# Softmax of differential attention over whole rows of scores, with the recurrent heads on one bank of PSUM

## The chip, the cores and the metric

The kernel runs on one core of a Trainium2 chip. The metric is the time of one execution on the device, in microseconds; a kernel's time is the median of its runs. Its engines are named as in the profile: PE (TensorE, matmuls; PEld is its weight load), DVE (VectorE), ACT (ScalarE), POOL (GpSimd) and SP (SyncE, which issues the DMAs). PSUM has eight banks; one bank holds 512 float32 columns of 128 rows.

## The reference

One encoder layer over two groups of rows, 2048 (prompt) and 256 (sample), width 1024. A projection feeds two mixers: differential attention with 4 heads, and a bidirectional recurrence (RWKV7) with 8 heads of 64. Their outputs are joined, projected (`w_out`), added to the input and passed through an MLP of width 4096. The part that the change touches:

```python
def one_block(q_blk):                                  # 128 queries, all keys of the sequence
    s = jnp.einsum("bqhcd,bkhcd->bhcqk", q_blk, k) * scale
    p = jax.nn.softmax(s, axis=-1)                     # c: the two maps of a head
    attn = p[:, :, 0] - lam * p[:, :, 1]
    return jnp.einsum("bhqk,bkhe->bqhe", attn, v)
o = rms_norm(o, subln_g) * (1.0 - lambda_init)
```

## The kernel before

`build` runs three stages: the projections with the recurrence's preparation, then attention and the recurrent units together, then `wout` and `mlp`. In the second stage `merge` pulls from two generators: one step of `attn_stream` (277 in all), then as many of `rw_units` (126) as keep pace. That gives the order of the program's text; a scheduling pass of the framework reorders instructions by its own timing of them and their priority, and then each engine executes its queue strictly in order. A tile from a pool with `bufs=n` has n slots; whoever needs a slot waits until its last reader is done.

`attn_stream` goes over 72 items: 4 heads, and in each 16 query tiles of the long sequence and 2 of the short one. A long item has 16 key tiles, in `nh` = 4 groups of `HB` = 4 tiles (512 columns). For each group and each of the two maps `attn_scores` (L581) does two matmuls into one bank `sc` (pool `asp`, `SC` = 3 slots of one bank), the negated maximum on DVE (L591) and the exponential on ACT with that group's own maximum as bias and the row sum as accumulator output (L595). Behind each group of scores stands `attn_pv` (L628) for the item before: four transposes into the one bank `atp` (L632), a copy on ACT (L634), and products with `vv` into `oo` (L637), whose one bank holds two items' outputs side by side.

Since each group has its own maximum, `attn_combine` (L598) makes up for it: the maximum over the groups (L604), the correction `cf` (L605, L606), corrected sums (L607, L608), the factor `g` of the second map for each group (L610 to L613). Then, for each group, it scales the first map's `P` by `cf` (L618 on ACT for the groups in `SCA`, L620 on POOL for the others) and adds the second map times `g` (L626 on DVE, or L623 and L624 on POOL for the groups in `STP`). `attn_out` (L639) norms the output: sum of squares on ACT (L643), two operations of one column on DVE (L645, L646), a power on POOL (L647), the scaling on DVE (L649), and the store.

The recurrent units: `rw_inter` (L875, once per unit and direction, 36 calls) makes from the prepared tensors the decays, the operands `ar` and `bk`, the scores `sc` (L935, evicted and masked by DVE at L938) and the transposed `bkt` (L941, evicted by ACT at L942); `rw_leaf` (L948) inverts small triangular blocks by 31 dependent steps (L962, L964) on DVE and POOL, between two transfers through DRAM (MD, XD); `rw_merge` (L968) puts the inverses together; `rw_chain` (L1025) runs the recurrence itself, whose output `yp` (L1016) is gathered over the whole of a step and copied by ACT (L1082). Its PSUM: the tag `w` with `WB` = 2 banks serves `lp` (L894), `scp`, `bp` and `yp`; the tag `ch` has one bank. So the eight banks are 3 for `sc`, one each for `atp` and `oo`, 2 for `w`, one for `ch`.

In `rw_inter` the scores take both banks at once:

```python
pss = [pp.tile([128, 4, 128], F32, name="scp", tag=SCPT, bufs=WB) for h in range(2)]
for c in range(4):
    for h in range(2):
        ...
        nc.tensor.matmul(pss[h][:, c], ...)
for h in range(2):
    nc.vector.tensor_tensor(out=sc[:, h, 4 * x:4 * x + 4], in0=pss[h], ...)
```

## Time and profile before

| | us |
|---|---|
| median of 3 runs (lowest, highest) | 4062.52 (4062.09, 4064.07) |
| the profiled execution | 4069.43 |
| its span, first to last instruction | 4067.6 |
| first and last score matmul (L588) begin at | 828.3 and 2170.1 |
| last product of attention (L637) begins at | 2193.7 |

| busy over the whole span | PE | PEld | DVE | ACT | POOL |
|---|---|---|---|---|---|
| us | 3841.0 | 3428.7 | 2535.4 | 1904.9 | 1249.5 |
| share | 94% | 84% | 62% | 47% | 31% |

The profile is of one execution. A share over the whole span mixes three stages; what concerns the change is read from the stretch between about 830 and 2195 us. PE's busy time is modelled from pipelined matmuls and contains some waiting; PEld beside it helps to judge it. A group's row gives busy time, the mean of one instruction, and the engine's idle time just before it with what ended that. The chain of waits is followed back from the last instruction, at each step to what released it or to the instruction before it on its engine.

### The profile page before, as it was taken

Reading aid. Unit: us, or ns where it says so; the run is one execution under the profiler, and the core shown is the slowest. Engines: PE = TensorE matmul, PEld = TensorE weight load, DVE = VectorE, ACT = ScalarE, POOL = GpSimd, SP = SyncE. Lnnn points to the kernel's source line nnn. Section 1 sums busy time; section 2 is a strip of 40 time slices with the busy share of each in tenths; the row PEclk is TensorE's granted clock in tenths of the full one; section 3 lists DMA queues with packets and bytes.
Section 4 is the critical chain, followed back from the end, with each engine's and each line's share of the span. In section 5 each row is a group of like instructions: output and inputs, shape, how many; then the busy total and the mean of one; then the engine's idle time right before and its main releaser. Section 6 shows DMA issues by size and latency. Waiting matters only on the chain.

```text
span 4067.6 us, 75970 instructions
## 1 busy us (share of the span) xinstructions
PE 3841.0 (94%) x28790; PEld 3428.7 (84%) x28790; DVE 2535.4 (62%) x5080; ACT 1904.9 (47%) x4312; POOL 1249.5 (31%) x1632
## 2 busy tenths in 40 slices
PE   8999998988889888889897999999999999999999
PEld 8999998976777677777776778999999999999998
DVE  4254767679878878788885775444444444444443
ACT  4354555467666656566665224333333333333332
POOL 0023666556656556556554440000000000000000
PEclk9999998999989989889998999999999999999999
DMA  6366666643443343334324376222252222521221
GB/s 188 121 198 194 199 178 195 181 108 73 111 95 83 94 119 90 85 85 112 89 62 151 105 234 200 63 68 67 63 186 63 64 66 65 158 63 63 63 63 39
DMA packets 617558, 458.05 MB, mean 113 GB/s; under 512 B 232498, under 2 KB 569191, under 8 KB 617192
## 3 DMA queue, kind: packets, MB, share of 16 engines
q1 hardware_dynamic: 617192, 453.20, 38.9%
q8 instruction: 227, 3.72, 0.4%
q14 instruction: 139, 1.14, 0.1%
HBM read 323.98 MB, written 129.07 MB: 111 GB/s over the span
## 4 chain that ended last, share of the span: by engine, by line
PE 54%; DVE 11%; POOL 6%; DMA 4%; issue 3%; ACT 2%; SPq 1%; POOLq 0%; DVEq 0%; ACTq 0%
PE ups L102 7%; PE ups L100 7%; PE ups L101 7%; PE yps L102 6%; PE yps L101 6%; PE yps L100 6%; DVE nb L591 2%; PE oo L637 2%; PE wops L101 2%; PE wops L100 2%; PE wops L102 2%; POOL lx L964 1%; DMA XD<-lx 1%; POOL ltmp L962 1%; DVE lx L964 1%
## 5 line engine op out<-in xcount | busy, mean ns | idle before, releaser
L504 DVE TENSOR_TENSOR acc<-yps,acc 128x512 f32<-128x512 f32 x576 | 392.0, 688 | 374.8 <-PE yps L102 374.8
L100 PE MATMUL ups<-h2hi,f_hi 128*128 128x384 f32 x1536 | 515.6, 336 | 0.0
L102 PE MATMUL ups<-h2hi,f_lo 128*128 128x384 f32 x1536 | 515.6, 336 | 0.0
L101 PE MATMUL ups<-h2lo,f_hi 128*128 128x384 f32 x1536 | 515.3, 335 | 0.0
L595 ACT ACTIVATE P<-sc,nb 128x512 f32<-128x512 f32 (+1 forms) x528 | 360.2, 685 | 218.4 <-DVE nb L591 203.2
L101 PE MATMUL yps<-f_lo,uh 128*128 128x512 f32 x1152 | 449.8, 391 | 0.0
L100 PE MATMUL yps<-f_hi,uh 128*128 128x512 f32 x1152 | 449.6, 391 | 0.0
L102 PE MATMUL yps<-f_hi,ul 128*128 128x512 f32 x1152 | 442.8, 391 | 0.0
L137 ACT CAST f_hi<-f_raw 128x1024 fp32r<-128x1024 f32 x96 | 96.2, 1048 | 646.7 <-PE yps L102 645.3
L591 DVE TENSOR_REDUCE nb<-sc 128x1 f32<-128x512 f32 (+1 forms) x528 | 345.2, 671 | 56.7 <-PE sc L589 55.6
L637 PE MATMUL oo<-vv,at 128*128 128x128 f32 x2080 | 307.0, 294 | 31.5 <-ACT at L634 20.6
L637 PEld LDWEIGHTS oo<-vv,at 128*128 128x128 f32 x2080 | 272.1, 202 | 60.9 <-ACT at L634 31.6
L588 PE MATMUL sc<-kt,qq 128*128 128x512 f32 (+1 forms) x528 | 253.3, 480 | 49.0 <-ACT P L595 42.1
L492 DVE TENSOR_TENSOR ul<-u,uh 128x384 fp32r<-128x384 f32 x192 | 106.8, 556 | 299.8 <-ACT uh L491 296.3
L101 PEld LDWEIGHTS ups<-h2lo,f_hi 128*128 128x128 f32 x1536 | 288.2, 188 | 5.7
L102 PEld LDWEIGHTS ups<-h2hi,f_lo 128*128 128x128 f32 x1536 | 288.2, 188 | 5.5
L100 PEld LDWEIGHTS ups<-h2hi,f_hi 128*128 128x128 f32 x1536 | 288.3, 188 | 5.5
L102 PEld LDWEIGHTS yps<-f_hi,ul 128*128 128x128 f32 x1152 | 216.1, 188 | 47.4
L143 DVE SCALAR_TENSOR_TENSOR f_lo<-f_raw,g,f_hi 128x256 fp32r<-128x256 f32 x384 | 168.7, 481 | 138.6 <-ACT f_hi L142 138.5
L100 PE MATMUL mm<-w_hi,hT_hi 128*128 128x256 f32 x864 | 250.2, 290 | 4.9 <-DVE qn L330 4.2
L100 PEld LDWEIGHTS yps<-f_hi,uh 128*128 128x128 f32 x1152 | 216.3, 188 | 39.3
L101 PE MATMUL mm<-w_lo,hT_hi 128*128 128x256 f32 x864 | 249.0, 289 | 0.0
(236 smaller groups left out, 9313.0 us busy)
## 6 DMA issues: line engine op xcount, KB each, us to landing
f_raw<-w_ff SPq DMA_DIRECT2D x192, 256.0 KB
f_raw<-w_ff SPq DMA_DIRECT2D x96, 512.0 KB
w_raw<-w_in SPq DMA_DIRECT2D x104, 256.0 KB
qq<-QT SPq DMA_DIRECT2D x288, 64.0 KB
kb<-KB SPq DMA_DIRECT2D x36, 512.0 KB
ZT<-zs SPq DMA_DIRECT2D x84, 192.0 KB
xt<-x SPq DMA_DIRECT2D x27, 512.0 KB
zr<-ZT SPq DMA_DIRECT2D x18, 516.0 KB
```

The source lines that it names most:

```text
L100: mm(ps, lh, rh, start=start, stop=False)
L101: mm(ps, lh, rl, start=False, stop=False)
L102: mm(ps, ll, rh, start=False, stop=stop)
L137: nc.scalar.copy(hi[:, ks], raw)
L143: nc.vector.scalar_tensor_tensor(out=lo[:, k], in0=raw[:, k - k0], scalar=gk, in1=hi[:, k].bitcast(F32), op0=ALU.mult, op1=ALU.subtract)
L492: nc.vector.tensor_tensor(out=ul[:, ns], in0=u2, in1=uh[:, ns].bitcast(F32), op=ALU.subtract)
L504: nc.vector.tensor_tensor(out=acc[j][:, cs], in0=ps, in1=acc[j][:, cs], op=ALU.add)
L588: nc.tensor.matmul(sc, qq[:, c, 0], kt, start=True, stop=False)
L591: nc.vector.tensor_reduce(out=m, in_=sc, axis=AX.X, op=ALU.max, negate=True)
L595: nc.scalar.activation(out=P, in_=sc, func=AF.Exp, bias=m, accum_out=(a["ls"][:, hf] if a["nh"] > 1 else a["l"])[:, c:c + 1])
L637: nc.tensor.matmul(a["op"], at[:, b], a["kv"][1][hf][:, b], start=k == 0, stop=k == a["n"] - 1)
L964: e.tensor_tensor(out=X[:, 0:i, k0:16], in0=X[:, 0:i, k0:16], in1=tmp[:, 0:i, 0:n], op=ALU.add)
```

## The change

Attention works on one map at a time over all its columns. `asp` gets two slots of two banks; `attn_scores(a, c)` fills both for map `c` (8 matmuls, 2048 columns), takes two maxima over 1024 columns and the minimum of the two negated values, and only then two exponentials of 1024 columns with the row's own bias. So nothing is rescaled: `cf` and all that makes and applies it is gone. `attn_combine` makes one factor `g` for the row; the first 512 columns are combined by DVE, the others of the second map are scaled by ACT in place and added by POOL, 512 columns at a time. In `attn_out` the two small operations go to POOL and the last scaling to ACT. `attn_pv` works as before on pieces of the wider tiles, and `attn_stream` puts two groups of products behind each map's scores. The probabilities are held in 4 and 2 tiles of 1024 columns (`PA`, `PB`) in place of 6 and 6 of 512.

Four banks for scores, with `atp`, `oo` and `ch`, leave one: `WB` becomes 1, and `rw_inter` does the scores of one half, evicts them, then the other half.

```diff
@@ attn_pools
-        self.asp = ctx.enter_context(tc.tile_pool(name="asp", bufs=SC, space=PSUM, side="right"))
+        self.asp = ctx.enter_context(tc.tile_pool(name="asp", bufs=2, space=PSUM, side="right"))
@@ attn_scores
-    def attn_scores(self, a, hf):
+    def attn_scores(self, a, c):
...
+        m = a["mx"] if nj > 1 else nb[:, :, 0]
+        scs = []
+        for j in range(nj):
+            sc = self.asp.tile([128, NB2, HW], F32, name="sc", tag="sc")
+            for b in range(NB2):
+                kt = a["kv"][0][c][j * NB2 + b]
+                nc.tensor.matmul(sc[:, b], qq[:, c, 0], kt, start=True, stop=False)
+                nc.tensor.matmul(sc[:, b], qq[:, c, 1], kt, start=False, stop=True)
+            sc = sc.rearrange("p b k -> p (b k)")
+            nc.vector.tensor_reduce(out=nb[:, c, j:j + 1], in_=sc, axis=AX.X, op=ALU.max, negate=True)
+            scs.append(sc)
+        if nj > 1:
+            nc.vector.tensor_reduce(out=m[:, c:c + 1], in_=nb[:, c], axis=AX.X, op=ALU.min)
+        for j in range(nj):
+            P = a["P"][c][j] = sp.tile([128, NB2 * HW], F32, name=f"P{c}", tag=f"P{c}", bufs=(PA, PB)[c])
+            nc.scalar.activation(out=P, in_=scs[j], func=AF.Exp, bias=m[:, c:c + 1],
+                                 accum_out=a["ls"][:, c, j:j + 1] if nj > 1 else a["l"][:, c:c + 1])
@@ attn_combine
...
+        if nj > 1:
+            nc.vector.tensor_reduce(out=l, in_=a["ls"], axis=AX.X, op=ALU.add)
+        nc.vector.reciprocal(g, l[:, 1:2])
+        nc.vector.scalar_tensor_tensor(out=g, in0=g, scalar=l[:, 0:1], in1=self.neglam, op0=ALU.mult, op1=ALU.mult)
+        for j in range(nj):
+            A, B = a["P"][0][j], a["P"][1][j]
+            k0 = 0
+            if j == 0:
+                nc.vector.scalar_tensor_tensor(out=A[:, 0:HW], in0=B[:, 0:HW], scalar=g, in1=A[:, 0:HW], op0=ALU.mult, op1=ALU.add)
+                k0 = HW
+            if k0 < NB2 * HW:
+                nc.scalar.activation(out=B[:, k0:], in_=B[:, k0:], func=AF.Copy, scale=g)
+            for k in range(k0, NB2 * HW, HW):
+                nc.gpsimd.tensor_tensor(out=A[:, k:k + HW], in0=A[:, k:k + HW], in1=B[:, k:k + HW], op=ALU.add)
@@ attn_out
-        nc.vector.scalar_tensor_tensor(out=rs, in0=l0, scalar=1e-6, in1=l0, op0=ALU.mult, op1=ALU.mult)
-        nc.vector.scalar_tensor_tensor(out=rs, in0=ss, scalar=1.0 / 128, in1=rs, op0=ALU.mult, op1=ALU.add)
+        nc.gpsimd.tensor_scalar(out=rs, in0=l0, scalar1=l0, scalar2=1e-6, op0=ALU.mult, op1=ALU.mult)
+        nc.gpsimd.tensor_scalar(out=rs, in0=ss, scalar1=1.0 / 128, scalar2=rs, op0=ALU.mult, op1=ALU.add)
...
-        nc.vector.tensor_scalar(out=o, in0=op, scalar1=rs, scalar2=None, op0=ALU.mult)
+        nc.scalar.activation(out=o, in_=op, func=AF.Copy, scale=rs)
@@ attn_stream
-            for hf in range(max(x["nh"] for x in (prev, cur) if x)):
-                if cur and hf < cur["nh"]:
-                    self.attn_scores(cur, hf)
-                if prev and hf < prev["nh"]:
-                    self.attn_pv(prev, hf)
-                yield
+            nh = max(x["nh"] for x in (prev, cur) if x)
+            for c in range(2):
+                if cur:
+                    self.attn_scores(cur, c)
+                for hf in range(c * nh // 2, (c + 1) * nh // 2) if nh > 1 else range(c):
+                    if prev and hf < prev["nh"]:
+                        self.attn_pv(prev, hf)
...
+                    yield
@@ rw_inter
-            pss = [pp.tile([128, 4, 128], F32, name="scp", tag=SCPT, bufs=WB) for h in range(2)]
-            for c in range(4):
-                for h in range(2):
-                    hs = slice(h * 64, h * 64 + 64)
...
+            for h in range(2):
+                hs = slice(h * 64, h * 64 + 64)
+                ps = pp.tile([128, 4, 128], F32, name="scp", tag=SCPT, bufs=WB)
+                for c in range(4):
+                    nc.tensor.matmul(ps[:, c], bk[hs, c, x].rearrange("p s t -> p (s t)"),
...
+                nc.vector.tensor_tensor(out=sc[:, h, 4 * x:4 * x + 4], in0=ps, in1=self.mask[:, d * (1 + h):d * (1 + h) + 1].to_broadcast([128, 4, 128]), op=ALU.mult)
@@ constants
-WB = 2
+WB = 1
-PA = 6
-PB = 6
+PA = 4
+PB = 2
```

## Rows read from the trace of the kernel before

**Rows 1.** windows, 900 to 2190 us: busy time of each engine (instructions), granted clock, DMA share, GB/s
```profile
900.00:2190.00 1290.00, 1136.99 (x13383) 944.54 (x13382) 1056.51 (x2398) 840.19 (x2098) 759.90 (x1125) 0.93 0.37 90
```

**Rows 2.** chain of waits, 900 to 2190 us, share by line, cut by the view
```profile
by line: issue 8.6%; DVE nb L591 6.9%; PE oo L637 5.0%; POOL lx L964 4.2%; DMA XD<-lx 4.1%; POOL ltmp L962 3.9%; DVE lx L964 3.7%; DVE ltmp L962 3.6%; DVE P L626 3.5%; POOL P L624 3.0%; PE scp L935 2.9%; PE sc L588 2.7%; PE atp L632 2.3%; A
```

**Rows 3.** groups by line, DVE, attention: busy us, mean ns | idle before, releasers
```profile
L591 DVE TENSOR_REDUCE nb<-sc 128x1 f32<-128x512 f32 x512 | 339.2, 679 | 52.4 <-PE sc L589 51.5
...
L591 DVE TENSOR_REDUCE nb<-sc 128x1 f32<-128x256 f32 x16 | 6.1, 411 | 4.3 <-PE sc L589 4.2
...
L626 DVE SCALAR_TENSOR_TENSOR P<-P,g,P 128x512 f32<-128x512 f32 (+1 forms) x136 | 135.3, 1029 | 2.9
...
L604 DVE TENSOR_REDUCE mx<-nb 128x2 f32<-128x8 f32 x64 | 9.5, 148 | 0.4
...
L605 DVE TENSOR_TENSOR cf<-mx,nb 128x8 f32<-128x8 f32 x64 | 13.4, 210 | 0.6
...
L607 DVE TENSOR_TENSOR ls<-ls,cf 128x8 f32<-128x8 f32 x64 | 17.6, 275 | 12.9 <-ACT cf L606 10.1 <-ACT P L595 2.2
...
L613 DVE TENSOR_SCALAR g<-cf,g 128x4 f32<-128x4 f32 x64 | 19.5, 304 | 1.0
...
L645 DVE SCALAR_TENSOR_TENSOR ors<-l 128x1 f32<-128x1 f32 x72 | 17.5, 244 | 0.1
...
L646 DVE SCALAR_TENSOR_TENSOR ors<-oss,ors 128x1 f32<-128x1 f32 x72 | 19.2, 267 | 18.5 <-ACT osq L643 18.1
...
L649 DVE TENSOR_SCALAR o<-oo,ors 128x128 f32<-128x128 f32 x72 | 24.6, 342 | 13.5 <-POOL ors L647 11.3 <-DMA MIX<-o 1.9
```

**Rows 4.** the same view, ACT
```profile
L595 ACT ACTIVATE P<-sc,nb 128x512 f32<-128x512 f32 (+1 forms) x528 | 360.2, 685 | 218.4 <-DVE nb L591 203.2 <-DVE P L626 4.6 <-POOL ors L647 3.6
...
L595 ACT ACTIVATION_READ_ACCUMULATOR P<-sc,nb 128x1 f32 x528 | 106.2, 201 | 0.0
...
L618 ACT ACTIVATE P<-P,cf 128x512 f32<-128x512 f32 x128 | 85.6, 717 | 1.4
...
L375 ACT ACTIVATE wo_hi<-acc,subg 128x1024 fp32r<-128x1024 f32 x4 | 4.6, 1149 | 4.0 <-DMA acc<-w_out 3.8
```

**Rows 5.** the same view, POOL
```profile
L624 POOL TENSOR_TENSOR P<-P,P 128x512 f32<-128x512 f32 x128 | 182.0, 1440 | 0.1
...
L623 POOL TENSOR_SCALAR P<-P,g 128x512 f32<-128x512 f32 x128 | 126.7, 1001 | 54.4 <-DVE g L613 35.8 <-DVE ors L646 9.3 <-ACT bkt L942 3.1
...
L620 POOL TENSOR_SCALAR P<-P,cf 128x512 f32<-128x512 f32 x128 | 98.3, 777 | 163.4 <-ACT cf L606 148.7 <-issue 9.9 <-ACT P L595 1.9
...
L647 POOL TENSOR_TENSOR ors<-ors,halfneg 128x1 f32<-128x1 f32 x72 | 42.6, 592 | 119.3 <-DVE ors L646 116.3 <-DVE lx L964 1.7 <-DVE g L610 0.8
```

**Rows 6.** waits, 828 to 2195 us: total us, times, longest us
```profile
PE sc L588 <- ACT P L595: 42.1, 35, 3.6
...
PE bp L941 <- DVE sc L938: 14.4, 13, 2.5
```

**Rows 7.** timeline, 1500 to 1545 us, rw_inter and one yp: start us, us, instruction
```profile
1511.25 0.91 PE L1016 MATMUL yp<-S,ar 64*64 64x64 f32 x22
...
1513.87 1.16 PE L894 MATMUL lp<-tw,wup 65*128 65x128 f32 x8
...
1525.22 0.56 ACT L1082 COPY ys<-yp 128x512 f32<-128x512 f32 x1
...
1530.74 1.16 PE L935 MATMUL scp<-ar,bk 64*128 64x128 f32 x16
...
1536.11 0.96 PEld L935 LDWEIGHTS scp<-ar,bk 64*128 64x128 f32 x8 [0.37 <-DVE zt L984]
...
1537.60 0.67 DVE L938 TENSOR_TENSOR sc<-scp,mask 128x512 f32<-128x512 f32 x1
...
1540.10 0.66 PE L941 MATMUL bp<-ident,bk 128*128 128x128 f32 x4
...
1541.15 0.59 ACT L942 COPY bkt<-bp 128x512 f32<-128x512 f32 x1
```

More of the change, by code (lines that the diff above doesn't have):

```diff
@@ L573, in attn_begin @@
                 nc.sync.dma_start(out=qq[64 * r:64 * r + 64, c].bitcast(F32), in_=self.QT[2 * h + c, :, :, t0:t0 + 128])
-        a = dict(h=h, t0=t0, HB=HB, nh=nh, n=n, kv=kv, qq=qq, P=[[None] * nh for _ in range(2)], op=self.oo[:, par])
-        for nm, shape in (("nb", [128, nh, 2]), ("ls", [128, nh, 2]), ("l", [128, 2]), ("g", [128, nh]), ("mx", [128, 2])):
+        a = dict(h=h, t0=t0, HB=HB, nh=nh, NB2=NB2, nj=nj, n=n, kv=kv, qq=qq, P=[[None] * nj for _ in range(2)], op=self.oo[:, par])
+        for nm, shape in (("nb", [128, 2, nj]), ("mx", [128, 2]), ("ls", [128, 2, nj]), ("l", [128, 2]), ("g", [128, 1])):
@@ L576, in attn_begin @@
             a[nm] = sp.tile(shape, F32, name=nm, tag="a" + nm)
[L577 to L578 removed]
         return a
[L581 removed]
+    def attn_scores(self, a, c):
         nc, sp = self.nc, self.aw
[L584 to L596 removed]
+        HW, nb, qq, nj, NB2 = a["HB"] * 128, a["nb"], a["qq"], a["nj"], a["NB2"]
+        m = a["mx"] if nj > 1 else nb[:, :, 0]
[15 more added lines that the diff above has]
+                                 accum_out=a["ls"][:, c, j:j + 1] if nj > 1 else a["l"][:, c:c + 1])
@@ L609, in attn_combine @@
-        gl = g[:, nh - 1:nh]
-        nc.vector.reciprocal(gl, l[:, 1:2])
-        nc.vector.scalar_tensor_tensor(out=gl, in0=gl, scalar=l[:, 0:1], in1=self.neglam, op0=ALU.mult, op1=ALU.mult)
-        if nh > 1:
-            nc.vector.tensor_scalar(out=g, in0=cf[:, :, 1], scalar1=gl, scalar2=None, op0=ALU.mult)
-        for hf in range(nh):
-            A = a["P"][0][hf]
-            if nh > 1 and not (RUN0 and hf == nh - 1):
-                if hf in SCA:
-                    nc.scalar.activation(out=A, in_=A, func=AF.Copy, scale=cf[:, hf, 0:1])
-                else:
-                    nc.gpsimd.tensor_scalar(out=A, in0=A, scalar1=cf[:, hf, 0:1], scalar2=1.0, op0=ALU.mult, op1=ALU.mult)
-            B = a["P"][1][hf]
-            if hf in STP:
-                nc.gpsimd.tensor_scalar(out=B, in0=B, scalar1=g[:, hf:hf + 1], scalar2=1.0, op0=ALU.mult, op1=ALU.mult)
-                nc.gpsimd.tensor_tensor(out=A, in0=A, in1=B, op=ALU.add)
-            else:
-                nc.vector.scalar_tensor_tensor(out=A, in0=B, scalar=g[:, hf:hf + 1], in1=A, op0=ALU.mult, op1=ALU.add)
+        nj, NB2, HW, l, g = a["nj"], a["NB2"], a["HB"] * 128, a["l"], a["g"]
@@ L628, in attn_pv @@
     def attn_pv(self, a, hf):
-        nc, HB, A = self.nc, a["HB"], a["P"][0][hf]
-        tp = (self.app if ATP else self.asp).tile([128, HB, 128], F32, name="atp", tag="atp" if ATP else "sc", bufs=ATP or SC)
+        nc, HB = self.nc, a["HB"]
+        A = a["P"][0][hf // a["NB2"]]
+        k0 = hf % a["NB2"] * HB * 128
+        tp = self.app.tile([128, HB, 128], F32, name="atp", tag="atp", bufs=ATP)
         for b in range(HB):
-            nc.tensor.transpose(tp[:, b], A[:, b * 128:b * 128 + 128], self.ident)
+            nc.tensor.transpose(tp[:, b], A[:, k0 + b * 128:k0 + b * 128 + 128], self.ident)
@@ L633, in attn_pv @@
         at = self.aw.tile([128, HB, 128], F32, name="at", tag="at", bufs=AT)
-        (nc.vector.tensor_copy if hf in ATV else nc.scalar.copy)(at, tp)
+        nc.scalar.copy(at, tp)
         for b in range(HB):
```

35 lines of the change are left out of this document (4 added, 31 removed).

## The prediction

> **What bounds the kernel now.** I read the windows first, then the chain of waits of the stretch in which attention runs, then the groups by line on each engine, the waits, and a short timeline. The change can only touch the stretch from about 830 to 2195 us, where attention and the recurrent heads run together; before it lie the projections, behind it the MLP's matmuls. In the 1290 us from 900 to 2190 no engine is full: PE is busy 88%, its weight loads 73%, DVE 82%, ACT 65%, POOL 59%, and the granted clock is 0.93, so PE spends a part of the stretch at the lower of its two levels [rows 1]. No engine's sum can simply be taken off the time. The chain of waits says how the time is put together: the reader should see that no line has more than 9% of it, that the score maxima (L591) have 6.9%, the combination on DVE (L626) 3.5%, the one on POOL (L624) 3.0%, and that much of the rest belongs to the recurrent heads: the leaf's lines L962 and L964 on both engines, its transfer (XD) and the score matmuls L935 [rows 2]. Attention and recurrence take turns in being late, and they meet in the queues of DVE and POOL.
>
> From this I take the rate at which work counts. L591 has 6.9% of 1290 us, 89 us, on the chain, of 345 us busy: 0.26. L626: 45 of 135 us, 0.33. L624: 39 of 182 us, 0.21 [rows 2, 3, 5]. A removed microsecond of DVE is thus worth about 0.27 us, one of POOL 0.21; for ACT the chain's row shows nothing, and since ACT is busy for 65% only [rows 1], I bound its rate by 0 and 0.2 and take 0.1.
>
> **The change part by part.** There are 64 long items (16 key tiles, 2048 scores a map) and 8 short ones (256 scores), which change little.
>
> DVE. The 512 maxima over 512 columns cost 0.679 us each, the 16 over 256 columns 0.411, so 0.268 us per 256 columns; a maximum over 1024 costs about 0.679 + 2 x 0.268 = 1.215 us, and 256 of them 311 us in place of 348: -37 us. Two minima over two values per item at the price of L604, 0.148 us, are 19 us where L604 had 9.5: +9.5. One of the two L626 of an item goes: 64 x 1.03 = -66 us. L605, L607 and L613 go (13.4 + 17.6 + 19.5 = -50 us). L645, L646 and L649 move to other engines (17.5 + 19.2 + 24.6 = -61 us) [rows 3]. Sum -205 us of DVE's busy time, at 0.27: -55 us.
>
> POOL. L620 and L623 go, 98 + 127 = -225 us. The sums L624 become three per item instead of two, 64 x 1.44 = +92 us. The 144 moved operations on one column have no row on POOL; L647, also one column wide, takes 0.592 us and bounds them from above, zero bounds them from below, and I take 0.45, nearer to that row: +65 us [rows 5]. Sum -68 us, at 0.21: -14 us.
>
> ACT. 512 exponentials with their accumulator reads cost 512 x (0.685 + 0.201) = 454 us; 256 over 1024 columns at 1.149 us, the price of an activation with a scale over 1024 columns (L375), and 256 reads are 346 us: -108 us. The scaling L618 (-86 us) is replaced by one of 512 and one of 1024 columns per item, now over the second map: 64 x (0.717 + 1.149) = +119 us. The last scaling arrives: 72 at no more than the 0.342 us that DVE takes for it, +25 us [rows 3, 4]. Sum -50 us, at 0.1: -5 us. Bounds 0 and -10.
>
> PE does the same matmuls, transposes and products, so its work doesn't change. The loads of queries and the stores of outputs keep their number and order on SP's queue; a store, and the recurrence's loads queued behind it, now wait for ACT's scaling in place of DVE's, and that for two operations on POOL that stand behind its sums (1.44 us each): I cost this at nothing, as long as the next item's scores cover it; each later microsecond per item would cost up to 72 us.
>
> So the relief is -74 us. Its ends: with a rate of 0.2 everywhere -65, with 0.33 on DVE and 0.2 on the others -91.
>
> Two costs stand against it. The first is the bank that the recurrent heads lose. Before, the scores of both halves go out in one burst of matmuls, two DVE evictions follow, and the transposes take the first bank that comes free; the six groups of a call of rw_inter took from 1530.74 to 1541.74 us, 11.0 us [rows 7]. After, each of six rounds (four times scores, twice transposes) must be evicted before PE may fill the only bank. With nothing else in the way, a score group is 0.96 us of PE and 0.67 of DVE, a transpose group 0.66 and 0.59 [rows 7]. With 0.15 us for each handover (an estimate from the gaps of these rows) a call is 4 x 1.93 + 2 x 1.55 = 10.8 us, where the old overlap, counted the same way, gives 7.0: 3.8 us more per call, 36 calls, 137 us. Behind a PE instruction that waits for the bank stand attention's matmuls, since PE takes its queue in order; the program's order can put others between, and that was mostly so before: PE stood 14.4 us in all for the transposes behind DVE [rows 6]. The bounds are 0 (always covered) and 137 (never). I take 0.27 of it, the rate that attention's lines on DVE have on the chain, since these rounds meet them in DVE's queue: +37 us.
>
> The second is the row maximum. No exponential starts before the maxima of both half rows and their minimum: 2 x 1.215 + 0.148 in place of 0.679 us, 1.9 us later in each of 128 maps, 243 us of latency. A map holds two slots of two banks, so the next map's matmuls start only behind its first exponential. Unhindered, a map takes about 0.9 us of matmuls, 2.6 of maxima, 1.15 of exponential and handovers, some 5.2 us, two of them 10.4 us of the 20 us that an item has (1290 / 64). So other work covers it, and the 42 us that PE stands today for a free score bank [rows 6] may fall (fewer, longer slots) or rise. Bounds -20 and +60 us; I take +10, near to what is there today.
>
> Sum: -74 + 37 + 10 = -27 us. The profiled execution took 4069.4 us, 1.8 us more than its span of 4067.6, and would come to 4042; the median of the runs, 4062.5, lies 6.9 us below that execution, and -27 on it gives 4035.
>
> One rule stands beside the row of L626. Its 1.03 us on average contrast with 0.67 us for a one-pass DVE instruction of the same width that reads PSUM (L938) [rows 3, 7]. The Trainium skill, page SBUF — State Buffer, section "Who interferes with whom", says that a DVE instruction with two SBUF inputs competes with a GpSimd instruction that reads SBUF. By it the L626 that is left stays slow as long as POOL's sums run beside it; if it ran free, the sum would be another 64 x 0.36 x 0.33 = 8 us lower.
>
> **The rivals.** (a) Slower: the one bank decides. Per unit of recurrence it would carry two calls, each with a first use of about 1.9 us (1.16 of matmuls from 1513.87 on, and an eviction) and the six rounds of 11.0 + 3.8 us, and two outputs yp, of which one held its bank from 1511.25 to 1525.78 us, 14.5 us [rows 7]: 2 x 16.7 + 2 x 14.5 = 62 us of a unit's 72 (1290 / 18). A bank in use 86% of the time leaves no room for anything to be late. If the 3.8 us are exposed in every call, the sum is -74 + 137 = +63: 4126 us. It decides from about half exposed, where 137 x 0.47 plus the 10 us eat the relief. For it: a call takes 28 us, from 1513.87 to 1541.74, so two fill 56 of the 72 us already. Against it: before, a call needed both banks at once, so an open yp barred it just as much, and DVE and POOL, which delay the evictions, are relieved. The Trainium skill, page Perfetto Trace Analysis, section "Identifying Performance Opportunities", says that the same gap coming back on an engine that should be full can mean that SBUF or PSUM has too little room for the next tile; this rival is that case, and its price is worked out above without the page.
> (b) More gain: both costs are covered. Then the relief at the rates above gives 4062 - 74 = 3988 us; at 0.5 for DVE, which is busiest after PE, -103 - 14 gives 3945.
> (c) No change: PE, whose work stays, is the true bound at 88% busy, or costs and relief are equal near half exposure: 4062 us, give or take 8.
>
> **How the numbers follow.** Forecast 4035 us with 0.35, case (b) 0.17, (c) 0.14, (a) 0.34. The likeliest case's own range is 4005 to 4054 (relief -91 to -65, the bank +20 to +50, the maximum 0 to +20). Both signs hold much of the chance, so the range that should hold 8 in 10 reaches from (b) into (a): 3955 to 4128. Within 0.2% (8 us, about what a measurement of this kernel can tell from no change) is case (c). Faster 0.52, same 0.14, slower 0.34.
>
> **What would show it.** Right: DVE's busy time in the stretch falls by some 200 us, ACT's and POOL's by 50 to 70, and the stretch becomes some 30 us shorter while PE's work stays. The maximum over 1024 columns should read near 1.2 us, the exponential near 1.15. PE's waits for evictions of the recurrent scores grow from 14 us to between 30 and 60. Case (a) would show as PE waits of over 100 us before the recurrent scores or transposes with DVE or ACT as releaser, and longer calls of rw_inter; case (b) as unchanged waits and PE over 90% busy. Wrong altogether would be a long new wait of ACT for POOL's sums (only two buffers hold the second map), behind which all its evictions queue, or a granted clock well below 0.93.

## The result and the profile after

The changed kernel takes 4227.81 us (median of 4 runs, 4211.47 to 4236.96), against 4063.26 us for the kernel before on the same chip: a ratio of 1.0401, with a 95% interval of 1.0368 to 1.0433. It is some 164 us slower; the forecast was 27 us faster, and the time lies outside the range. The profiled execution took 4229.14 us with a span of 4227.2, 159.6 us more than that of before.

First the windows of the kernel after: the stretch of [rows 1], and 100 us from its end (length, then busy time and instructions of PE, PEld, DVE, ACT, POOL; granted clock, DMA share, GB/s).

```profile
900.00:2190.00 1290.00, 1122.29 (x12036) 951.87 (x12034) 880.33 (x1669) 794.01 (x1592) 627.88 (x1013) 0.91 0.35 86
...
2200.00:2300.00 100.00, 60.44 (x780) 52.19 (x776) 36.71 (x86) 19.56 (x39) 17.33 (x39) 0.63 0.24 56
```

In the same 1290 us PE gets through 12036 matmuls where it had 13383 [rows 1], and DVE, ACT and POOL all have more idle time: the relief is there, and yet the whole is slower. The second row shows where the time appears. Attention is done early: its last product begins at 2148 us (2194 before). The recurrence is not: its last output is copied at 2370 us (2201 before). For 220 us it runs alone; in the 100 us shown PE is 60% busy and the granted clock is 0.63, between the two levels.

Next the groups by line of the kernel after, 828 to 2360 us (count | busy us, mean ns of one | idle before and releasers), with the prices that the forecast had to guess.

```profile
L595 DVE TENSOR_REDUCE nb<-sc 128x1 f32<-128x1024 f32 x256 | 309.6, 1217 | 120.2 <-PE sc L593 119.4
...
L601 ACT ACTIVATE P<-sc,mx 128x1024 f32<-128x1024 f32 x256 | 283.7, 1113 | 72.3 <-DVE mx L598 69.3 <-POOL ors L643 1.1 <-POOL tt L983 0.9
...
L621 POOL TENSOR_TENSOR P<-P,P 128x512 f32<-128x512 f32 x192 | 253.3, 1344 | 87.1 <-ACT P L619 71.6 <-PE atp L629 10.7 <-PE sc L593 4.2
...
L938 DVE TENSOR_TENSOR sc<-scp,mask 128x512 f32<-128x512 f32 x144 | 99.0, 688 | 153.5 <-PE scp L936 152.3
...
L616 DVE SCALAR_TENSOR_TENSOR P<-P,g,P 128x512 f32<-128x512 f32 x64 | 65.7, 1026 | 0.8
...
L942 ACT COPY bkt<-bp 128x512 f32<-128x512 f32 x72 | 42.5, 590 | 76.5 <-PE bp L941 76.2
L643 POOL TENSOR_SCALAR ors<-oss,ors 128x1 f32<-128x1 f32 x72 | 27.8, 386 | 118.0 <-ACT osq L640 117.4
...
L642 POOL TENSOR_SCALAR ors<-l 128x1 f32<-128x1 f32 x72 | 21.9, 304 | 249.4 <-DVE l L609 236.3 <-ACT o L646 6.5 <-ACT en L905 5.5
```

The maximum over 1024 columns takes 1.217 us (1.215 expected), the exponential 1.113 (1.149), a one-column operation on POOL 0.304 or 0.386 (0.45). The idle time before L938 is the reading to keep: DVE stands 152 us for the recurrent scores of PE, and ACT 76 us for the transposes.

The matmuls of the recurrent scores, before (828 to 2195 us) and after (828 to 2360 us), show one thing more:

```profile
L935 PE MATMUL scp<-ar,bk 64*128 64x128 f32 x1152 | 139.1, 303 | 18.3 <-POOL bk L922 7.8 <-DVE bk L927 4.5 <-ACT bkt L942 3.8
...
L936 PE MATMUL scp<-ar,bk 64*128 64x128 f32 x1152 | 194.9, 318 | 34.6 <-DVE bk L928 16.5 <-DVE sc L938 10.8 <-ACT bkt L942 5.4
```

The same 1152 matmuls keep PE busy 56 us longer. Before, where the two halves alternate, 45% of them begin within 60 ns of a neighbour, so that the two halves (64 rows each) run side by side: 16 in 1.16 us [rows 7]. After, none do, and 8 take 1.16 us.

The waits view says which side waits: before (828 to 2148 us, as long as both kernels have attention running),

```profile
PE sc L588 <- ACT P L595: 41.5, 34, 3.6
ACT bkt L942 <- PE bp L941: 27.9, 24, 2.9
DVE sc L938 <- PE scp L935: 14.7, 17, 2.0
PE bp L941 <- DVE sc L938: 14.4, 13, 2.5
```

and after, over the same 1320 us (total us, times, longest us):

```profile
DVE sc L938 <- PE scp L936: 113.1, 68, 5.4
PE sc L592 <- ACT P L601: 44.0, 35, 6.1
ACT bkt L942 <- PE bp L941: 34.6, 24, 5.8
...
PE scp L936 <- DVE sc L938: 7.1, 5, 2.6
PE scp L936 <- ACT bkt L942: 4.0, 2, 3.6
```

PE waits for evictions of the one bank for only 7.1 + 4.0 us, less than the 14.4 that it waited before for the transposes alone. The order of the program puts attention's matmuls into the gaps. It is the evicting engines that wait, for recurrent matmuls that stand in PE's queue behind attention's. A timeline of the kernel after shows both forms of a call's score phase, one beside attention from 1342.90 us, one in the lone tail from 2201.51 us (start us, us, instruction, [idle before it and its releaser]):

```profile
1342.90 1.16 PE L936 MATMUL scp<-ar,bk 64*128 64x128 f32 x8
1344.25 0.68 DVE L938 TENSOR_TENSOR sc<-scp,mask 128x512 f32<-128x512 f32 x1
...
1347.27 1.16 PE L936 MATMUL scp<-ar,bk 64*128 64x128 f32 x8
1348.46 0.69 DVE L938 TENSOR_TENSOR sc<-scp,mask 128x512 f32<-128x512 f32 x1 [1.46 <-PE scp L936]
...
1350.76 0.60 PE L941 MATMUL bp<-ident,bk 128*128 128x128 f32 x4
1351.39 0.59 ACT L942 COPY bkt<-bp 128x512 f32<-128x512 f32 x1 [3.15 <-PE bp L941]
...
1352.63 1.16 PE L936 MATMUL scp<-ar,bk 64*128 64x128 f32 x8
1353.82 0.69 DVE L938 TENSOR_TENSOR sc<-scp,mask 128x512 f32<-128x512 f32 x1
...
1356.90 1.16 PE L936 MATMUL scp<-ar,bk 64*128 64x128 f32 x8
1358.10 0.69 DVE L938 TENSOR_TENSOR sc<-scp,mask 128x512 f32<-128x512 f32 x1 [2.61 <-PE scp L936]
...
1360.49 0.60 PE L941 MATMUL bp<-ident,bk 128*128 128x128 f32 x4
...
1363.02 0.59 ACT L942 COPY bkt<-bp 128x512 f32<-128x512 f32 x1
...
1364.51 1.05 PE L895 MATMUL lp<-tw,wup 65*128 65x128 f32 x8
...
2201.51 2.07 PE L936 MATMUL scp<-ar,bk 64*128 64x128 f32 x8 [1.40 <-DVE bk L928]
2203.62 0.69 DVE L938 TENSOR_TENSOR sc<-scp,mask 128x512 f32<-128x512 f32 x1 [2.16 <-PE scp L936]
2204.37 2.07 PE L936 MATMUL scp<-ar,bk 64*128 64x128 f32 x8 [0.78 <-DVE sc L938]
...
2215.87 0.59 ACT L942 COPY bkt<-bp 128x512 f32<-128x512 f32 x1 [6.91 <-PE bp L941]
2216.51 1.97 PE L1016 MATMUL yp<-S,ar 64*64 64x64 f32 x32 [0.68 <-ACT bkt L942]
```

Alone, a round goes from one score group to the next in 2.86 us (2201.51 to 2204.37), its matmuls slowed by the low clock. With the 1.16 us that the same group takes at the higher level it would be 1.95, and the forecast had 1.93 for a round with nothing in the way. Beside attention a round takes 4.4 us (1342.90 to 1347.27): the eviction ends at 1344.93, the bank is free, and the next group begins 2.3 us later. At 1364.51, 0.9 us after the last copy, the next call starts. The two outputs yp begin at 2216.51, directly behind the last copy: they too need this bank.

From here on calls are counted over the trace's list of instructions. A call runs from its first matmul lp to the end of its second copy bkt; its score phase is the part from the first scp on. A unit is two calls; the gap is from the end of the second call to the next unit's first lp. Call, score phase and gap are means of all 36 calls or 18 units; the unit's length is the mean distance of the starts of units 3 to 15, so that it differs a little from the sum of its parts. The last two columns are the starts of the last product of attention and of the last copy ys. What is left of a unit lies between its two calls: 0.4 us before and 1.0 after, but 9.0 in e11, while in e7 the two overlap by 7.3. All in us.

| kernel | ratio to before [95%] | call | score phase | gap | unit | last oo | last ys |
|---|---|---|---|---|---|---|---|
| before | 1 | 28.5 | 13.7 | 12.3 | 71.2 | 2193 | 2201 |
| after | 1.0401 [1.0368, 1.0433] | 34.4 | 20.2 | 11.1 | 83.0 | 2148 | 2370 |
| e1_one_bank | 1.0498 [1.0476, 1.0520] | 35.5 | 20.8 | 9.7 | 84.4 | 2071 | 2399 |
| e2_halves_two_banks | 1.0134 [1.0113, 1.0156] | 31.5 | 13.7 | 9.1 | 74.5 | 2245 | 2253 |
| e11_bp_own | 1.0187 [1.0168, 1.0206] | 23.6 | 8.4 | 18.0 | 75.4 | 2231 | 2267 |
| e12_yp_own | 1.0339 [1.0304, 1.0375] | 38.0 | 22.4 | 1.5 | 80.7 | 2184 | 2341 |
| e5_yp_late_ch | 1.0271 [1.0253, 1.0289] | 37.0 | 21.2 | 0.9 | 78.3 | 2239 | 2303 |
| e13_one_bank_yp_late | 1.0377 [1.0359, 1.0395] | 38.7 | 22.8 | 1.1 | 80.4 | 2175 | 2357 |
| e8_before_yp_ch | 1.0065 [1.0050, 1.0080] | 34.3 | 13.7 | 1.5 | 71.2 | 2196 | 2225 |
| e7_bp_yp_ch | 1.0475 [1.0460, 1.0491] | 40.1 | 15.1 | 6.9 | 84.5 | 2096 | 2390 |
| e4_shared | 1.0650 [1.0624, 1.0676] | 24.4 | 11.1 | 38.8 | 91.8 | 2066 | 2466 |
| e6_chain_first | 1.0714 [1.0696, 1.0731] | 33.7 | 19.9 | 20.5 | 90.9 | 2056 | 2490 |
| e3_rate | 1.0407 [1.0385, 1.0428] | 34.2 | 19.9 | 11.0 | 83.3 | 2145 | 2363 |
| e18_before_rate | 1.0087 [1.0072, 1.0103] | 28.1 | 13.3 | 9.0 | 68.0 | 2233 | 2131 |
| e17_sc2_wb3 | 1.0245 [1.0221, 1.0269] | 26.3 | 10.9 | 18.1 | 73.8 | 2289 | 2238 |
| e14_no_dve_combine | 0.9972 [0.9960, 0.9984] | 29.1 | 13.1 | 10.1 | 71.5 | 2171 | 2182 |
| e10_out_moved | 1.0014 [1.0005, 1.0024] | 30.2 | 13.4 | 8.8 | 70.1 | 2187 | 2193 |
| e9_lw_own | 1.0175 [1.0160, 1.0190] | 29.5 | 13.2 | 13.2 | 77.2 | 2254 | 2262 |
| e15_no_transposes | 1.0047 [1.0031, 1.0063] | 30.7 | 13.6 | 8.5 | 71.8 | 2189 | 2210 |
| e16_whole_rows_two_banks | 1.0081 [1.0056, 1.0106] | 31.3 | 15.4 | 10.1 | 73.6 | 2208 | 2230 |

The account of the change in this table: the score phase is 6.5 us longer and the call 5.9. The two calls of a unit stand behind one another, and 2 x 5.9 = 11.8 us is the growth of the unit from 71.2 to 83.0, the gap being a little shorter. This adds up where the time lies; it is no law. In e8 a call is 5.8 us longer than before and the unit is the same, and in e11 the calls are 11.9 us shorter than in e1 and the unit only 9.0: the calls, the gap and the time between calls trade with one another. Over the whole recurrence, from the first call's start to the last call's end, it is 204 us (1241 before, 1445 after). The first call starts 9 us earlier, and what follows the last call is 26 us shorter (79 instead of 105): 204 - 9 - 26 = 169, the shift of the last ys from 2201 to 2370.

### The profile page after: what moved, and what is told of

It reads as the page before. It is cut to its first block, busy times and chain, and to the rows that moved or that the text cites. A ratio compares the mean times of both kernels' runs of the same rounds, so it can differ in the third digit from the quotient of the medians.

```text
span 4227.2 us, 74765 instructions
## 1 busy us (share of the span) xinstructions
PE 3910.4 (93%) x28790; PEld 3512.3 (83%) x28790; DVE 2389.8 (57%) x4416; ACT 1877.6 (44%) x3808; POOL 1133.8 (27%) x1584
## 5 line engine op out<-in xcount | busy, mean ns | idle before, releaser
L595 DVE TENSOR_REDUCE nb<-sc 128x1 f32<-128x1024 f32 (+1 forms) x272 | 316.1, 1170 | 127.3 <-PE sc L593 126.5
L601 ACT ACTIVATE P<-sc,mx 128x1024 f32<-128x1024 f32 x256 | 283.7, 1113 | 72.3 <-DVE mx L598 69.3
L621 POOL TENSOR_TENSOR P<-P,P 128x512 f32<-128x512 f32 x192 | 253.3, 1344 | 87.1 <-ACT P L619 71.6
```

The costliest lines, as they stand in the source:

```text
L595: nc.vector.tensor_reduce(out=nb[:, c, j:j + 1], in_=sc, axis=AX.X, op=ALU.max, negate=True)
L601: nc.scalar.activation(out=P, in_=scs[j], func=AF.Exp, bias=m[:, c:c + 1], accum_out=a["ls"][:, c, j:j + 1] if nj > 1 else a["l"][:, c:c + 1])
L621: nc.gpsimd.tensor_tensor(out=A[:, k:k + HW], in0=A[:, k:k + HW], in1=B[:, k:k + HW], op=ALU.add)
```

## The experiments

Kernels were compared in several groups, each with runs of the kernel before of its own (medians of 4059.5 to 4063.3). Differences between two experiments are therefore taken between their ratios, times 4061 us.

**The bank alone, the order alone.** The first takes the recurrent half of the change and leaves attention as it was; the second only the order in which the halves are done, on two banks.

```diff
 # e1_one_bank, from before: rw_inter as in the change (one half, evict, other half), and
-WB = 2
+WB = 1
 # e2_halves_two_banks: rw_inter as in the change, WB stays 2
```

> The kernel before, attention untouched; only the recurrent heads get the change: WB = 1 and the scores of one half evicted before the other half's matmuls (the bank set free stays empty). Theory 1 (the bank): losing it slows the recurrence by itself, whatever attention does; then most of the 164 us show here, 4170 to 4230 us, with the last yp copy 100 us or more behind the last product of attention. Theory 2 (the pace): the lighter, wider attention runs ahead and the recurrence is left over at the end; the bank by itself costs little, 4060 to 4100 us.

Measured 1.0498, +202 us: more than the whole change costs, with attention as it was. The bank, with the order that it forces, is the cause, and whole rows give 39 us of it back (1.0498 to 1.0401).

> The kernel before with the order of rw_inter's score matmuls alone changed (one half, its eviction, the other half), two banks kept. Both theories: within 20 us of 4063, since each half may take its own bank; if it came out over 4100, the order of the matmuls and not the number of banks would be the cost in the changed kernel.

Measured 1.0134, +54 us with the score phase unchanged at 13.7 us; the call grew to 31.5. With one bank the old order isn't possible, since it fills two banks before it empties one, so the price of the bank contains that of the order: 202 = 54 for the order and 148 for the room, if the order costs as much with one bank as with two. The share of score matmuls that begin beside a neighbour falls from 45% to 21% in e2, and they keep PE busy 156.7 us instead of 139.1. That may be a part of the 54 us; no run tests it apart.

**What the one bank does.** It holds lp, four score groups and two groups of transposes per call, and two outputs yp per unit. Both of the next kernels start from e1, and use the bank that e1 leaves free for one of these.

```diff
 # e11_bp_own, from e1
-            bp = pp.tile([128, 4, 128], F32, name="bp", tag="w", bufs=WB)
+            bp = pp.tile([128, 4, 128], F32, name="bp", tag="bp", bufs=1)
 # e12_yp_own, from e1
-            yp = pp.tile([128, 2, 4, 64], F32, name="yp", tag=YPT, bufs=WB if YPT == "w" else CH)
+            yp = pp.tile([128, 2, 4, 64], F32, name="yp", tag="yo", bufs=1)
```

> The kernel before with one bank w (as the run of one bank alone, 4262 us) and the bank set free given to the transposes bp of rw_inter alone: four rounds of a call share w, not six. Theory 1b (the rounds): the score phase falls from 20.8 us to 14 to 16 and most of the loss comes back, 4070 to 4150 us. Theory 1a (yp shut out between calls): the calls shorten a little, the loop stays, 4190 to 4250 us.

> As before, but the bank set free goes to yp alone. Theory 1a: yp no longer waits for the calls, the gap of 9.7 us between units goes and a unit takes 71 to 75 us: 4070 to 4130 us. Theory 1b: calls stay at 35 us and the six rounds at 20: a unit of no less than 71 us, and the time 4170 to 4240 us if the gap has another cause.

A bank for the transposes gives back 126 us (1.0498 to 1.0187): the score phase falls to 8.4 us, below that of before. A bank for yp gives back 65 us (to 1.0339): the score phase is no shorter (22.4), but the gap falls from 9.7 to 1.5 us and the unit from 84.4 to 80.7: yp no longer has to be put between the units. These are two different costs of one bank, and together 191 of its 202 us, though they were not tried together and need not add. The waits of e1, while attention runs (828 to 2071 us),

```profile
DVE sc L937 <- PE scp L935: 37.6, 39, 6.7
ACT bkt L941 <- PE bp L940: 11.1, 14, 1.9
```

say something else besides: with the old attention DVE stands for the scores only 37.6 us, not 113, probably since it has more other work to fill the time with, and yet the score phase is as long (20.8). The waits of an engine don't measure the rounds. Their parts do: by the list of instructions, while attention runs, the next group of matmuls begins on average 1.38 us after the eviction's end in e1 and 1.51 after the change, and DVE's eviction begins 0.70 and 0.30 us after the matmuls' end. Most of the delay lies in PE's queue, with either attention.

**Making room after the change.** Three ways to keep whole rows and take load off the bank: yp is put behind the state's update and into `ch`; with it the transposes too; or `w` and `ch` become one pool of two banks.

```diff
 # e5_yp_late_ch, from after: the first products of yp, and its tile, stand behind the update of S
-YPT = "w"
+YPT = "ch"
 # e7_bp_yp_ch: e5, and
-            bp = pp.tile([128, 4, 128], F32, name="bp", tag="w", bufs=WB)
+            bp = pp.tile([128, 4, 128], F32, name="bp", tag="ch", bufs=CH)
 # e4_shared, from after: mp, qp, up and dS from "ch" to
-        mp = pp.tile([128, 2, 8, 32], F32, name="mp", tag="ch", bufs=CH)
+        mp = pp.tile([128, 2, 8, 32], F32, name="mp", tag="w", bufs=2)
...
-WB = 1
+WB = 2
```

> The changed kernel, but the recurrence's output yp is gathered in one go behind dS and in the bank of tag ch, so that the single bank w serves rw_inter alone. In the changed kernel two calls of rw_inter of 34.4 us follow each other, then a gap of 11.1 us in which both yp are made, 83.0 us a unit (before: 28.5, 28.5 and 12.3, 71.2 us). Theory 1a (the loop): the gap exists because yp gets the bank only between calls and the next unit's calls wait for what the chain frees; then the gap shrinks to a few us, a unit takes 70 to 74 us, and the time is 4030 to 4090 us. Theory 1b (the rounds): only the longer calls count, and the gap, which was there before with two banks as well, stays; 4190 to 4240 us.

> As the run with yp late in ch, and the transposes bp of rw_inter in the bank ch too: the bank w then has four rounds in a call and not six. Theory 1b (the rounds): the score phase falls from 20 us to about 14, a call to 28 us, and the time by 18 x 12 us, to 4000 to 4060 us. Theory 1a: as without this edit or, since ch is now also shared, up to 60 us worse than that run.

> The changed kernel with the recurrence's two banks as one pool: what had the tag ch (mp, qp, up, dS) takes the tag w, two slots for all. Theory 1 (the bank): a call of rw_inter may use two banks again while no step of the chain holds them, so a part comes back: 4100 to 4180 us. Theory 2 (the pace): nothing changes, 4210 to 4240 us.

The first gives 53 us (1.0401 to 1.0271), and the gap goes from 11.1 to 0.9 us, as with e12: the outputs' share of the bank's price is shown twice, with either attention. The second shortens the score phase to 15.1 but makes the calls longer (40.1, of which 25.0 ahead of the first scp) and the whole worse (1.0475); that the transposes now share `ch` with the state's chain is the likely reason, which no run tests. The shared pool has the shortest calls of all with whole rows (24.4) and the longest gap (38.8), at 1.0650. Moving the wait from one part of the unit to another is easy; it is the unit that counts.

**The same move where there is room.** yp in `ch` on the kernel before, and on e1:

```diff
 # e8_before_yp_ch, from before; e13_one_bank_yp_late, from e1: the edit of e5
-YPT = "w"
+YPT = "ch"
```

> The kernel before with yp gathered behind dS in the bank ch: its calls of rw_inter then have both banks to themselves. Theory 1a (the loop): the gap of 12.3 us between units shrinks here too and the time falls by 50 us or more, to 3950 to 4010 us. Theory 1b: calls stay at 28.5 us and the time within 25 us of 4062.

> The attention of the kernel before with the recurrence of the run with yp late in ch (one bank w; that run, with whole-row attention, took 4174 us). Theory R (whole rows relieve DVE, ACT and POOL and this counts also where both streams end together): slower than that run by 20 to 80 us, 4190 to 4250. Theory 0 (the relief counts only by shortening the recurrence's queueing; attention itself is as long): 4165 to 4185 us. Slower whole rows (4174 would then be the worse one): under 4160 us.

With two banks the move costs 26 us (1.0065). The gap falls here too, from 12.3 to 1.5 us, and yet the unit stays at 71.2, because the calls grow by as much, all of it ahead of the score phase. A shorter gap is thus no gain by itself. What follows the last call is 10 us longer. So the move is no improvement of its own but relief for a bank that is short. On e1 it gives 49 us (1.0498 to 1.0377). The comparison of e13 with e5, the same recurrence with old and new attention, repeats the 39 us from above: 1.0377 against 1.0271, 43 us for whole rows while there is one bank.

**Order.** Two changes of the order of the text after, and one of before: more recurrence ahead of attention (`RATE`), and the chain first in each step.

```diff
 # e3_rate, from after; e18_before_rate, from before
-RATE = 1.0
+RATE = 1.4
 # e6_chain_first, from after
-MORD = "icm"
+MORD = "cim"
```

> The changed kernel with RATE 1.4 in place of 1.0: the recurrence's instructions stand earlier in the program relative to attention's, nothing else. Theory 2 (the pace): the recurrence no longer ends 220 us behind attention, and the time comes back to 4030 to 4100 us. Theory 1 (the bank): calls of rw_inter stay long, the recurrence still sets the end, 4170 to 4230 us.

> The kernel before with RATE 1.4: the same instructions, the recurrence's earlier in the program's order. It shows what an order of the queues alone moves. If order is nearly free, within 10 us of 4060; if the engines' orders are the cause of the 50 us that the order of the score matmuls alone cost, a shift of 20 us or more to either side. In the changed kernel the same edit gave no difference.

> The changed kernel with the chain of a unit placed ahead of the next calls of rw_inter in the program's order (MORD cim in place of icm). Theory 1a (the loop): yp then goes ahead of the calls for the bank, the loop is opened at another place, and 40 to 120 us come back: 4110 to 4190 us. Theory 1b (the rounds): the calls stay as long, 4200 to 4250 us.

After the change a higher rate does nothing: 4223.6 us at 1.0407, unit 83.3. An earlier place in the text does not make the recurrence faster there, so that a wrong pace between the two streams is not the cause of the loss. Before, it does: with 1.4 the unit falls to 68.0 and the last ys comes at 2131 us, but attention then ends at 2233 instead of 2193, and the whole is slower by 0.9%. Before, the two streams end together, and here one gains at the other's cost. The chain first is worse (1.0714, gap 20.5).

**The split the other way.** Two banks for attention's scores, three for the recurrent heads, all else as before:

```diff
 # e17_sc2_wb3, from before
-WB = 2
+WB = 3
-SC = 3
+SC = 2
```

> The kernel before with one bank moved the other way: two slots for scores instead of three, three banks w. If a bank is worth more to the recurrence than to attention in general, faster by 20 to 80 us: 3980 to 4040. If the second bank was the one that counts (two halves at once) and the third adds nothing, while attention loses a slot, slower: 4065 to 4130 us.

Calls of 26.3 us and a score phase of 10.9, but attention ends at 2289 us (2193 before): 1.0245. Of the splits that were tried, three for attention's scores and two for the recurrent heads is the best; a bank less costs either side.

**What relief is worth.** Three kernels measure the other half of the sum on the kernel before, with two banks. One leaves out DVE's combination; one moves the three operations of `attn_out` as the change does; one gives `lw` a buffer of its own, for which the first map's probabilities lose one.

```diff
 # e14_no_dve_combine, from before
-                nc.vector.scalar_tensor_tensor(out=A, in0=B, scalar=g[:, hf:hf + 1], in1=A, op0=ALU.mult, op1=ALU.add)
+                pass
 # e10_out_moved, from before: the three lines of attn_out as in the change
 # e9_lw_own, from before
-        lw = sp.tile([128, 512], F32, name="lw", tag="bk", bufs=1)
+        lw = sp.tile([128, 512], F32, name="lw", tag="lw", bufs=1)
-PA = 6
+PA = 5
```

> The kernel before, leaving out the combination on DVE (L626) of two of the four groups (their weights are then the first map's alone): 131 us of DVE's busy time less in the stretch, and nothing else. By the rate of the prediction (0.27) 4060 - 35 = 4025 us; with the 0.33 of L626's own share of the chain 4017. If relief of DVE counts for nothing while the recurrence has its two banks, 4045 to 4075 us.

> The kernel before with the change's part in attn_out alone: two small operations from DVE to POOL, the last scaling from DVE to ACT, 61 us of DVE's busy time less. By the rate of the prediction (0.27 of DVE's, 0.21 of POOL's busy time) 4062 - 16 + 14 = 4060 us; if DVE is the bound, 4000 to 4030 us; by theory 3 within 20 us of 4062, since no step of a call becomes shorter.

> The kernel before with its two banks; lw gets a tile of its own in place of sharing bk's (paid for with one buffer fewer of the first map's probabilities, PA 5), so that a call of rw_inter can begin while the one before it is in its score phase. Theory 3 (the calls of rw_inter, one behind the other, set the pace of the kernel before as well, so that attention's work on DVE counts only where it delays a call): a unit falls below 70 us and the time by 40 us or more, to 3950 to 4020. Rival (no line sets the pace, engines do): 4040 to 4080 us.

Without its 135 us of L626 the kernel, which then also frees two of the second map's tiles sooner, gains 10.5 us (0.9972 [0.9960, 0.9984]): 0.08 of the busy time, not 0.27, and far less than the 45 us that L626 had on the chain [rows 2]. The chain of waits of e14, 900 to 2190 us, shows why (share by line, cut by the view):

```profile
by line: PE oo L637 7.8%; DVE nb L591 6.4%; issue 6.3%; PE scp L935 5.8%; DVE ltmp L962 5.2%; DVE lx L964 5.2%; PE sc L588 3.7%; DMA xt<-XD 3.1%; PE atp L632 3.0%; PE sc L589 2.8%; DMA XD<-lx 2.4%; POOL lx L964 2.4%; POOL ltmp L962 2.3%; DM
```

L626 is gone, and its place on the chain is taken by lines that were there beside it: PE's L637 from 5.0 to 7.8%, L935 from 2.9 to 5.8%, the leaf's DVE lines from 3.6 and 3.7 to 5.2% each [rows 2]. Moving 61 us off DVE gives nothing (1.0014 [1.0005, 1.0024], 6 us slower). The kernel with `lw` apart missed: the calls are no shorter, the unit is longer, attention ends at 2254 us. It changes two things at once, the buffer for `lw` and the one less for P, so its cause stays open.

**Whole rows with two banks.** There is no ninth bank; to have four for scores and two for the recurrent heads, attention's transposes and with them the bank `atp` must go. Both attentions were run in that form, with ACT copying P itself to `at`.

```diff
 # e15_no_transposes, from before; e16_whole_rows_two_banks the same from after, with WB = 2 and rw_inter of before
-        tp = (self.app if ATP else self.asp).tile([128, HB, 128], F32, name="atp", tag="atp" if ATP else "sc", bufs=ATP or SC)
-        for b in range(HB):
-            nc.tensor.transpose(tp[:, b], A[:, b * 128:b * 128 + 128], self.ident)
...
-        (nc.vector.tensor_copy if hf in ATV else nc.scalar.copy)(at, tp)
+        nc.scalar.copy(at, A.rearrange("p (b k) -> p b k", b=HB))
```

> The kernel before, leaving out the PE transposes of the attention weights (the copy to at reads the weights in SBUF untransposed, so the products are not the reference's); the bank of atp is then empty. It is the reference point of the next run. 1040 transposes of about 0.11 us of PE less: 4000 to 4062 us by either theory.

> The changed kernel, leaving out the same transposes, and with the empty bank given to the recurrent heads: WB = 2 and rw_inter as before. So it is whole-row attention with nothing taken from the recurrence, to be compared with the run before it. Theory R: faster than that run by 30 to 110 us (the relief of 74 us of the prediction, give or take). Theory 0: within 20 us of it. A slower result by over 20 us means that the later first exponential and the two slots cost more than all the relief.

Old attention 1.0047 [1.0031, 1.0063], whole rows 1.0081 [1.0056, 1.0106]: 14 us more, with intervals that touch. The windows of e15, 900 to 2190 us (columns as above),

```profile
900.00:2190.00 1290.00, 1071.22 (x12312) 871.03 (x12314) 1073.75 (x2379) 840.30 (x2081) 756.13 (x1120) 0.87 0.37 89
```

and of e16

```profile
900.00:2190.00 1290.00, 1053.85 (x12129) 880.93 (x12129) 933.71 (x1782) 814.63 (x1629) 677.16 (x1077) 0.88 0.37 89
```

show that DVE is relieved by 140 us and POOL by 79, and the time isn't better. So where the recurrent heads have two banks, whole rows as they stand, the relief and the later first exponential together, are worth nothing that these runs can tell. The pair has a limit: e15 itself is slower than before though it leaves work out, and its granted clock is 0.87 where before has 0.93 [rows 1].

None of these kernels beats the one before, but for e14, which leaves out part of the sum. The nearest with whole rows is e5, still 2.7% slower.

## Why the prediction was wrong

**The step that failed is the term of the bank, +37 us**, worked out as 3.8 us a call, times 36 calls, times 0.27. It measured +202 us for the bank alone. Three things in it were off; that PE's work would not change was wrong as well, since the recurrent score matmuls keep PE busy 56 us longer.

The 3.8 us. The rounds were counted with nothing else in the way, 10.8 against 7.0 us. Alone that holds: 1.95 us a round by the timeline of the tail. But the work that stands in the same queues adds to each handover. By the table the score phase takes 13.7 us before, 6.7 more than the 7.0, and 20.2 after, 9.4 more than the 10.8. Taking the old order as four steps in series (a burst with its evictions, a group of transposes, and both again) and the new one as six, that is 1.7 and 1.6 us a step: on this reading the queue's price is the same, and it is paid twice more. The rows would have given it: the one call read in [rows 7] took 11.0 us, which is already 4 more than the unhindered 7.0.

The 0.27. This was attention's rate on the chain, applied to work that isn't attention's. Even with yp out of its way (e12) the one bank cost 138 us, as much as the 137 that were counted at the most, and not 0.27 of that. A call is part of the recurrence, whose calls followed one another closely: the second call of a unit began on average 0.4 us behind the first. The forecast had this in hand, since rival (a) counted two calls of 28 us in a unit of 72, and used it for the room in the bank and not for the rate. Between before and after the unit grew by as much as its two calls, 2 x 5.9 = 11.8 us. What a microsecond of a call is worth in general these runs don't show: shorter by 11.9 us each in e11, the two calls gave 9.0 us a unit.

What was not in the term at all. The outputs yp: they were counted as load on the bank, in rival (a), but the price of being shut out until a unit's calls are over (65 us by e12, 53 by e5) was in no sum.

**Rival (a)** had the mechanism, "the one bank decides", with 0.34, and a price of +63 us in place of +164, since it took the same 3.8 us and none for yp. Its sign in the profile was wrong too: PE waits of over 100 us before the recurrent scores were expected, and while attention ran PE waited 11 us. PE's queue, filled from two streams, showed few such waits; the engines behind it had them (113 us of DVE), and the calls got longer. "Longer calls of rw_inter" was the sign to trust. The Trainium skill, page Perfetto Trace Analysis, section "Optimizing Tensor Performance", says under "Matmuls" that independent groups of matmuls should rotate through different PSUM banks, so that the emptying of one overlaps the next group's matmuls. These runs agree: giving the transposes a bank of their own to alternate with is worth 126 us. The rule that the forecast did cite from the same page, on the gap that keeps coming back, looks at the engine that should be full. The cause that it names was there, but the trace does not show its sign: PE, 87% busy in the stretch after the change, waited 11 us for the bank.

**The relief, -74 us, was too large, though DVE's part of it was sized right.** The durations agreed, and the rows of DVE's groups add up to 2732 us before and 2525 after, -207 (-205 expected); the busy time in section 1 of the page fell by 146 for DVE, 27 for ACT (50 expected) and 116 for POOL (68 expected). The rate was wrong. A line's share of the chain says how often it came last, not what is won when it goes: e14 gives 0.08 for L626 where its share gave 0.33, because the chain closes over the next line. With two banks whole rows brought nothing (e16 against e15). With one bank they bring 39 to 43 us, in two pairs. The calls get shorter with it: 35.5 us in e1 and 34.4 after, 36 x 1.1 = 40 us in all, and the shorter delay at DVE (0.70 to 0.30 us) goes along. But the 17 gaps take 17 x 1.4 = 24 us of that back, and from the first call to the last the recurrence is 20 us shorter (1465 and 1445); it also starts 8 us earlier. That relief of DVE counts where the calls are long is a reading that fits; no run tests it apart. The rule of the Trainium skill beside L626, page SBUF — State Buffer, section "Who interferes with whom", held on both sides. L616 is on average as slow as before (1.026 us); by the list of instructions after, the 17 of the 64 beside which hardly any POOL instruction ran took 0.749 us, and the 21 that had POOL beside them throughout 1.515 (means). Without the combination on DVE, POOL's sums in e14 (828 to 2195 us) are faster than the 1.440 us of [rows 5]:

```profile
L624 POOL TENSOR_TENSOR P<-P,P 128x512 f32<-128x512 f32 x128 | 170.1, 1347 | 0.1
```

**The row maximum, +10 us,** was not measured by itself. Its sign was right: PE's wait for a free score bank was 41.5 us and is 44.0. ACT had no long wait for POOL's sums, though its last scaling in `attn_out` waited 33.6 us in all (828 to 2360 us) for POOL's power, which was put at nothing; e10, with the same move, is 6 us slower than before.

**The clock** is read here as a consequence; no run tests it apart. It is 0.91 in the stretch, and falls to 0.63 between 2200 and 2300 us, after attention's matmuls are gone; a score group then takes 2.07 us instead of 1.16. That makes the lone tail longer, and is then part of the bank's price.

**Left open:** how much of the 1.3% that the order of the halves alone costs with two banks comes from the matmuls that no longer run side by side, when the score phase stays as it was (e2); what e9 lost; why leaving out the transposes makes the kernel slower at a lower clock (e15).

## What to carry to other kernels

When a loop loses a buffer, count the serial steps that it adds, and price each at what a step takes in the loaded queue, read from many rounds of the trace, not at its unhindered sum. Then see whether the loop's rounds stand back to back: if they do, little of that is hidden, however idle the engines look. It is not one for one: a gap beside a step can grow as the step gets shorter (e11), and only a run tells by how much. A line's share of the chain of waits is no rate at which its removal pays; a kernel that leaves the line out measures it, here 0.08 against 0.33.

## What the runs showed of the hardware

- A queue filled from two streams hid the cost of a scarce buffer from the waits of its own engine: while attention ran, PE waited 11 us for the one bank, and the calls took 36 x 5.9 = 212 us more.
- An engine that gets less to do need not make the kernel faster even at 82% busy [rows 1]: 135 us off DVE gave 10.5 us, 61 us gave none.
- The granted clock was lower where PE had less work: 0.63 in the lone tail, where PE was 60% busy, and 0.87 without the transposes, with 1071 us busy of 1290, against 0.93 with 1137 [rows 1].
- Matmuls of 64 rows on the two halves of PE ran side by side when the text alternated between the halves: 16 in 1.16 us [rows 7], against 8 in 1.16 us when each half went out alone.
- An operation on DVE with two inputs in SBUF (L616) took 0.749 us where POOL was idle beside it, and 1.515 us where POOL worked throughout.
